# A seventh up group by seven products, the residual's turn on two queues, and a partial sum in free banks of the last round

## The chip, the cores and the metric

The kernel runs on one core of a Trainium2 chip. The metric is device time in microseconds (us) of one execution; lower is better. The engines are TensorE (PE), VectorE (DVE), ScalarE (ACT), GpSimd (POOL) and SyncE (SP). DMAs are issued here from SP's queue, from GpSimd's and, rarely, from ScalarE's.

## The reference

Two residual layers on 512 rows of width 1024 in float32: a mixer (banded attention in layer 0, a gated linear recurrence in layer 1), then a dense MLP. Only the MLP is touched:

```
def sq_relu_mlp(h, w1, w2):
    z = jax.nn.relu(jnp.einsum('bsd,df->bsf', h, w1))
    return jnp.einsum('bsf,fd->bsd', z * z, w2)

for layer in range(DEPTH):
    hn = rmsnorm(h, norm_mix[layer])
    ...
    h = h + mix
    h = h + sq_relu_mlp(rmsnorm(h, norm_mlp[layer]), mlp_w1[layer], mlp_w2[layer])
return rmsnorm(h, norm_final)
```

w1 is 1024 x 4096 and w2 4096 x 1024, each 16 MB, so an MLP reads 32 MB of weights.

## The kernel before

**A product.** Every float32 matmul is made of three (mm3, L273 to L276): high by high part (L274), low by high (L275), high by low (L276). Weights come by DMA into raw tiles, and each is split into a high part `wh` by a cast on ScalarE (L178) and a low part `wl` by a subtraction on VectorE (L181). The split parts live in a ring of five.

**The planner.** `plan` is a list of weight pieces in the order of use. `want` (L210) hands out the next piece and first calls `fetch` (L152) for the next three or four. `fetch` issues the DMA of a plain piece, makes the sums of weights that a piece needs, splits it, and, keyed by the kind of the piece, issues the loads of later pieces (`load_up`, `load_down`). So the place of a piece in the plan sets both when its casts and when later loads are issued.

**Seven products.** A group of 512 features is the product of two 2 x 2 block matrices, and `group` (L764 and after) computes it by seven block products instead of eight, in the order u11, us1, us2, u12, us3, us4, u22. The blocks of w1 are 512 x 256. us1 is the sum of two blocks and is made by a load and a load that accumulates, issued on GpSimd (L136, `kept` tiles). us2 is made on VectorE from u11 and us1. us3 is the block u11 with a block accumulated on it by a DMA of GpSimd (L163); it can be issued once us2 has read u11. us4 is made on VectorE (L166). Each product is 24 matmuls of 128x256. The copies `S.copy(b6, b1)`, `S.copy(v, b5)` and `S.copy(u, b6)` stand between them: b6 starts as a copy of b1 after the first product, and the third and later products accumulate on it.

**Down products.** The down side of a round p takes two groups (1024 features) and is made by seven products as well, named by their weights 11, t1, 22, 21, t2, t3, t4 in the plan and 11, s1, s4, 12, s2, s3, 22 by their activations in `round_`. Sums of blocks of w2 are made by DMAs b<-b on GpSimd (L123, L174). The activations are sums too, made by `opening` and `sums`, and split by `split` (L851 on ScalarE, L852 on VectorE). `read` (L741) adds a finished bank to the residual d on VectorE, scaled by the row's factor `rq` or `nrq`.

**The order of an MLP.** (1) Eight plain columns, `up(0, 0)` to `up(0, 7)`, 1024 features. Each is 24 matmuls of 128x512, two relus and two squares on ScalarE (L754, L755). (2) Rounds 0 to 3. In rounds 0 to 2 each of the seven down products is followed by two of the fourteen up products of the next round's two groups. Round 3 has no up products. Its end is `turns` (layer 0) or `ends` (layer 1).

**What lies between the columns.** After column 0, `turn` (L723) transposes the residual on VectorE into two tiles `turned` (L727) and sends 32 DMAs of 64 KB to d, all on SP (L734). After the columns 1 to 5 the operands of the groups are scaled and split (`scaled`, `right`, `right_split`). After column 5 the eight squares of d (`squares`, L949, 128x512 with a row sum) give the lengths of the rows, and after column 6 rq is made from them. The loads for round 0 and the next group are issued after the columns 4 to 6.

In round 3 the step 11 writes banks X; after s4 the kernel copies X to Y (`S.copy(Y[t], X[t])`, L899), since step 12 goes on in Y what 11 began, while s2 goes on in X. Y is read before that for s1 and s4.

Of the kernel before, what the change touches and what calls it, by code (L numbers as in the profile page):

```python
# [40 lines left out]
def trunk(ctx: ExitStack, tc: tile.TileContext, xT, cols, gfin, win, wqkv, wo, rwin, rga, rgx, rwo, w1, w2, out):  # L41
# [10 lines left out]
    def mmp(name):  # L52
        return ps.tile([P, T], F32, name=name, tag="mm")
# [66 lines left out]
    def first_sum(key):  # L120
        if key in down:
            for h in range(2):
                G.dma_start(raws["12", h], raws["11", h], accum_op=ALU.add)  # L123
# [14 lines left out]
    def fetch():  # L138
        i = state["next"]
        state["next"] += 1  # L140
        kind, nk, key = plan[i]
        H = wsp.tile([P, 1024], F32R, name=f"wh{i}", tag="wh")
        L = wsp.tile([P, 1024], F32R, name=f"wl{i}", tag="wl")
        n, half = 1024, nk
        if kind[:5] == "plain":
            n = nk * sum(src.shape[1] for src in key)
            raw = wraw.tile([P, 1024], F32, name=f"wr{i}", tag=f"wr{state['plain'] % 3}")
            state["plain"] += 1
            rv = raw[:, :n].rearrange("p (k c) -> p k c", k=nk)
            c0 = 0  # L150
            for n_, src in enumerate(key):
                w = src.shape[1]  # L152
                queue = nc.scalar if i == 0 and n_ else nc.sync
                queue.dma_start(rv[:, :, c0 : c0 + w], rows(src))
                c0 += w
        elif kind[0] == "u":
            nk = 4
            following = (key[0], key[1] + 1)
            if kind == "us2":
                raws["us2"] = wraw.tile([P, 1024], F32, name=f"us2_{key[0]}{key[1]}", tag=f"wr{(state['base'] + 2) % 3}")  # L160
                V.tensor_add(raws["us2"], raws["u11"], raws["us1"])
                raws["us3"] = raws["u11"]
                G.dma_start(four(raws["us3"]), rows(upper[key]["21"]), accum_op=ALU.add)  # L163
            if kind == "us4":
                raws["us4"] = raws["u12"]
                V.tensor_add(raws["us4"], raws["us4"], raws["us2"])  # L166
            raw = raws[kind]
        else:
            nk = 2
            following = (key[0], key[1] + 1)  # L170
            raw = raws[{"t1": "12", "t2": "22", "t3": "11", "t4": "21"}.get(kind, kind), half]
            if kind == "t2":
                V.tensor_add(raw, raw, raws["12", half])
                G.dma_start(raws["21", half], raw, accum_op=ALU.add)  # L174
            if kind == "t3":
                V.tensor_sub(raw, raws["22", half], raw)
        if i:
            S.copy(H[:, :n], raw[:, :n])  # L178
        else:
            start_.append(V.tensor_copy(H[:, :n], raw[:, :n]))  # L180
        low = V.tensor_sub(L[:, :n], raw[:, :n], f(H[:, :n]))  # L181
        if not i:
            start_.append(low)
        if kind == "plain_":
            state["base"] = state["plain"] % 3
            load_up((nk_layer[i], 0), "11")
            load_up((nk_layer[i], 0), "12")
        elif kind == "us2":
            load_up(following, "s1")
        elif kind == "us3":  # L190
            load_up(following, "11")
        elif kind == "us4":
            load_up(following, "12")
        elif kind == "u22":
            load_up(following, "22")
        elif kind == "t2" and half:
            load_down(following, "12")
        elif kind == "t3" and half:
            load_down(following, "11")
        elif kind == "t4" and half:  # L200
            first_sum(following)
            load_down(following, "22")
            load_down(following, "21")
        state["ready"].append((nk, H[:, :n].rearrange("p (k c) -> p k c", k=nk), L[:, :n].rearrange("p (k c) -> p k c", k=nk)))
# [31 lines left out]

    def add_mlp(layer):
        starts.append(len(plan))
        for j in range(KT):
            plan.append(("plain" if j < KT - 1 else "plain_", KT, [w1[layer][:, j * P : (j + 1) * P]]))  # L240
        nk_layer[len(plan) - 1] = layer
        for n in range(6):
            c0 = (n + 2) * T
            upper[layer, n] = {
                f"{i + 1}{j + 1}": w1[layer][j * T : (j + 1) * T, c0 + i * U : c0 + (i + 1) * U]
                for i in range(2) for j in range(2)
            }
        for p in range(4):
            down[layer, p] = {
                f"{k + 1}{c + 1}": w2[layer][(2 * p + k) * T : (2 * p + k + 1) * T, c * T : (c + 1) * T]  # L250
                for k in range(2) for c in range(2)
            }
            ups = [("u" + n, 4, (layer, 2 * p + g)) for g in range(2) for n in ("11", "s1", "s2", "12", "s3", "s4", "22")]
            for n, kind in enumerate(("11", "t1", "22", "21", "t2", "t3", "t4")):
                plan.extend((kind, half, (layer, p)) for half in range(2))
                if p < 3:
                    plan.extend(ups[2 * n : 2 * n + 2])
# [409 lines left out]
    def mlp(ly, norm):  # L667
        with ExitStack() as mctx:
# [54 lines left out]
            def turn():  # L723
                blocks = [sr.tile([P, 2, 4, KT, 32], F32, name=f"turned{ly}{h}", tag=f"b{n}2") for h, n in enumerate((1, 2))]
                for k in range(KT):
                    for h in range(2):
                        V.transpose(  # L727
                            blocks[h].rearrange("p t j k a -> p (t j) k a")[:, :, k],
                            hT[k][:, h * U : (h + 1) * U].rearrange("p (n b) -> p n b", b=32),
                        )  # L730
                for h in range(2):
                    for i in range(4):
                        for j in range(4):
                            nc.sync.dma_start(  # L734
                                res[32 * j : 32 * j + 32, 2 * h : 2 * h + 2, i // 2, (i % 2) * U : (i % 2 + 1) * U],
                                blocks[h][32 * i : 32 * i + 32, :, j].rearrange("p t k a -> p t (k a)"),
                            )
# [8 lines left out]
            def up(p, j):  # L746
# [15 lines left out]
                    for n in (1, 3, 2, 4):  # L762
                        right(n)
                if j == 3:  # L764
                    right_split(1)
                    right_split(3)
                if j == 4:
                    right_split(2)
                    opening(0)
                    load_down((ly, 0), "11")  # L770
                if j == 5:
                    right_split(4)
                    state["kept"] = per.tile([P, 2, 1024], F32, name=f"kept{ly}", tag="hx1")
                    load_up((ly, 0), "s1")
                    load_down((ly, 0), "12")
                    first_sum((ly, 0))
                if j == 5:
                    for t in range(4):
                        for c in range(2):
                            squares(t, c)  # L780
                if j == 6:
                    load_up((ly, 0), "22")
                    load_down((ly, 0), "22")
                    load_down((ly, 0), "21")
                    V.tensor_add(rq, fs[:, 0:8:2], fs[:, 1:8:2])
                    V.tensor_scalar(rq, rq, 1.0 / D, EPS, ALU.mult, ALU.add)
                    V.reciprocal(rq, rq)
                    V.tensor_scalar(nrq, rq, -1.0, None, ALU.mult)

            def group(p, g):  # L790
                def piece(bank, op, fresh):
# [81 lines left out]
            def round_(p):  # L873
# [16 lines left out]
                def step(name, bank, fresh, t0, c):  # L890
                    if p < 3:
                        product(name, bank, fresh)
                    for t in range(2):
                        if p == 3:
                            product(name, bank, fresh, ts=(t,))
                        if name != "11":
                            read(bank[t], t0 + t, c)
                        if name == "s4":
                            S.copy(Y[t], X[t])  # L899
                    give(low[name][1])  # L900

                ups = (x for g in range(2) for x in group(p + 1, g)) if p < 3 else iter(range(14))
# [1 line left out]
                def rise(n):  # L904
                    for _ in range(n):
                        next(ups)

                step("11", X, True, 0, 0)
                rise(2)
                split("s4", p)  # L910
# [3 lines left out]
                step("s4", Y, False, 0, 1)  # L914
                rise(2)
                split("s2", p)
                step("12", Y, False, 0, 0)
                rise(2)
                split("s3", p)
                step("s2", X, False, 0, 1)  # L920
# [120 lines left out]
                S.activation(dt[3, 1][:, HI], dt[3, 1][:, HI], AF.Copy, scale=total(3))  # L1041
                store(3, 1, nc.scalar)

            for j in range(KT):
                up(0, j)
            sums(0, False)
            sums(0, True)
            for p in range(4):
                round_(p)
            state["ahead"] = 4  # L1050
# [208 lines left out]
```

## Time and profile before

| | us |
|---|---|
| median of 3 runs | 1042.24 (1040.31 to 1042.85) |
| the profiled execution | 1041.71 |
| its span | 1039.9 |
| TensorE busy | 1025.5 (99%) |
| VectorE busy | 863.0 (83%) |
| ScalarE busy | 659.3 (63%) |
| GpSimd busy | 68.7 (7%) |

The mean granted clock of TensorE is 0.997 of full speed. The plain columns of layer 0 run from 244.61 to 288.15. A row of the timeline gives the start, the duration, the engine with the line, and the operation; in brackets stands the idle time of the engine before it and what ended that. Matmuls overlap in the pipeline, so the price of one is the distance of starts (or a window's length divided by its count), not its own duration.

### The profile page before, as it was taken

Reading aid. Unit: us, or ns where it says so; the run is one execution under the profiler, and the core shown is the slowest. Engines: PE = TensorE matmul, PEld = TensorE weight load, DVE = VectorE, ACT = ScalarE, POOL = GpSimd, SP = SyncE. Lnnn points to the kernel's source line nnn. Section 1 sums busy time; section 2 is a strip of 40 time slices with the busy share of each in tenths; the row PEclk is TensorE's granted clock in tenths of the full one; section 3 lists DMA queues with packets and bytes.
Section 4 is the critical chain, followed back from the end, with each engine's and each line's share of the span. In section 5 each row is a group of like instructions: output and inputs, shape, how many; then the busy total and the mean of one; then the engine's idle time right before and its main releaser. Section 6 shows DMA issues by size and latency. Waiting matters only on the chain.

```text
span 1039.9 us, 14946 instructions
## 1 busy us (share of the span) xinstructions
PE 1025.5 (99%) x5618; PEld 890.4 (86%) x5618; DVE 863.0 (83%) x1216; ACT 659.3 (63%) x1024; POOL 68.7 (7%) x84
## 2 busy tenths in 40 slices
PE   9999999999999999999999999999999999999997
PEld 8888888888889999999988788888889999999985
DVE  7998778969479889689699989988289789789697
ACT  7666556647556567566557686656566566566565
POOL 1000000000111111111000000000111111011000
PEclk9999999999999999999999999999999999999999
DMA  8444354243768738837613422173758738737413
GB/s 273 114 127 137 82 158 126 62 140 98 226 123 222 194 71 220 205 61 202 183 21 94 141 68 73 51 222 104 235 107 223 203 62 222 203 62 202 122 41 102
DMA packets 126248, 145.22 MB, mean 140 GB/s; under 512 B 6240, under 2 KB 98400, under 8 KB 126176
## 3 DMA queue, kind: packets, MB, share of 16 engines
q1 hardware_dynamic: 108320, 114.18, 35.4%
q0 software_dynamic: 17280, 29.36, 16.5%
q8 instruction: 44, 0.72, 0.3%
q10 hardware_dynamic: 576, 0.72, 0.2%
q14 instruction: 28, 0.23, 0.1%
HBM read 116.98 MB, written 2.10 MB: 115 GB/s over the span
## 4 chain that ended last, share of the span: by engine, by line
PE 82%; DVE 9%; DMA 4%; issue 2%; SPq 2%; ACT 1%; DVEq 0%; POOL 0%; ACTq 0%; POOLq 0%
PE m L276 8%; PE m L275 8%; PE m L274 8%; PE x L274 4%; PE x L275 4%; PE x L276 4%; PE y L276 4%; PE y L274 4%; PE y L275 4%; DVE wl L181 3%; DMA b<-b 2%; PE x L500 2%; PE wo L274 1%; PE wo L275 1%; PE ro L275 1%
## 5 line engine op out<-in xcount | busy, mean ns | idle before, releaser
L181 DVE TENSOR_TENSOR wl<-b,wh 128x1024 fp32r<-128x1024 f32 x112 | 136.3, 1223 | 42.8 <-ACT wh L178 42.5
L178 ACT CAST wh<-b 128x1024 fp32r<-128x1024 f32 x112 | 117.1, 1051 | 85.7 <-PE m L275 44.2
L276 PE MATMUL m<-rH,wl 128*128 128x256 f32 x384 | 108.6, 283 | 0.0
L275 PE MATMUL m<-rL,wh 128*128 128x256 f32 x384 | 108.6, 283 | 0.0
L274 PE MATMUL m<-rH,wh 128*128 128x256 f32 x384 | 108.6, 283 | 0.0
L178 ACT CAST wh<-wr 128x1024 fp32r<-128x1024 f32 (+1 forms) x73 | 75.0, 1031 | 45.2 <-PE wo L275 11.7
L181 DVE TENSOR_TENSOR wl<-wr,wh 128x1024 fp32r<-128x1024 f32 (+1 forms) x74 | 87.8, 1190 | 16.0 <-ACT wh L178 15.6
L276 PE MATMUL m<-hnH,wl 128*128 128x256 f32 x288 | 81.6, 283 | 0.0
L275 PE MATMUL m<-hnL,wh 128*128 128x256 f32 x288 | 81.6, 283 | 0.0
L274 PE MATMUL m<-hnH,wh 128*128 128x256 f32 x288 | 81.4, 283 | 0.0
L275 PEld LDWEIGHTS m<-rL,wh 128*128 128x128 f32 x384 | 73.7, 192 | 1.2
L274 PEld LDWEIGHTS m<-rH,wh 128*128 128x128 f32 x384 | 73.6, 192 | 1.2
L276 PEld LDWEIGHTS m<-rH,wl 128*128 128x128 f32 x384 | 73.6, 192 | 0.0
L178 ACT CAST wh<-u 128x1024 fp32r<-128x1024 f32 x48 | 50.4, 1050 | 27.8 <-PE x L276 16.5
L181 DVE TENSOR_TENSOR wl<-u,wh 128x1024 fp32r<-128x1024 f32 x48 | 58.6, 1221 | 4.1 <-ACT wh L178 4.1
L275 PEld LDWEIGHTS m<-hnL,wh 128*128 128x128 f32 x288 | 55.2, 192 | 0.7
L274 PEld LDWEIGHTS m<-hnH,wh 128*128 128x128 f32 x288 | 55.1, 191 | 0.7
L276 PEld LDWEIGHTS m<-hnH,wl 128*128 128x128 f32 x288 | 55.2, 192 | 0.0
L274 PE MATMUL y<-wh,hs 128*128 128x512 f32 x128 | 50.6, 395 | 1.8 <-DVE d L741 1.4
L274 PE MATMUL x<-wh,h 128*128 128x512 f32 (+1 forms) x132 | 50.9, 386 | 1.3 <-DVE d L1030 1.3
L276 PE MATMUL y<-wh,ls 128*128 128x512 f32 x128 | 50.2, 392 | 1.9 <-DVE ls L852 1.9
L276 PE MATMUL x<-wh,l 128*128 128x512 f32 (+1 forms) x132 | 50.9, 385 | 0.0
(373 smaller groups left out, 2964.5 us busy)
## 6 DMA issues: line engine op xcount, KB each, us to landing
b<-in_w SPq DMA_DIRECT2D x64, 512.0 KB, 5.8
b<-b POOLq DMA_DIRECT2D x32, 512.0 KB, 7.3
u<-in_w SPq DMA_DIRECT2D x24, 512.0 KB, 5.0
kept<-in_w SPq DMA_DIRECT2D x24, 512.0 KB, 5.3
wr<-in_wqkv SPq DMA_DIRECT2D x20, 512.0 KB, 4.1
wr<-in_w SPq DMA_DIRECT2D x16, 512.0 KB, 4.3
wr<-in_rwin SPq DMA_DIRECT2D x16, 512.0 KB, 4.0
kept<-in_w POOLq DMA_DIRECT2D x12, 512.0 KB, 5.9
```

What stands on the lines that cost most here:

```text
L178: S.copy(H[:, :n], raw[:, :n])
L181: low = V.tensor_sub(L[:, :n], raw[:, :n], f(H[:, :n]))
L274: PE.matmul(acc, WH, XH, start=start, stop=False, skip_group_check=more)
L275: PE.matmul(acc, WH, XL, start=False, stop=False, skip_group_check=more)
L276: PE.matmul(acc, WL, XH, start=False, stop=stop, skip_group_check=more)
L500: PE.transpose(b[:, c : c + P], pt[:, seg[t] + kt * P : seg[t] + (kt + 1) * P], ident)
```

## The change

1. The second 512 features are no longer four plain columns but a group of seven products, `group(0)`. The plan has four plain columns, then the seven pieces, then the rounds; the groups of the rounds are numbered one higher. The fourth column is now `plain_`, so u11 and u12 of group 0 are loaded before the MLP begins. us2 and u22 of group 0 no longer load the next group's first pieces; a new function `first` does, and it also issues the loads of the down weights between the pieces.
2. All four `right_split` come after column 3. The squares and rq go into `lengths`, called at the end of `first`, after the group and the first sums.
3. `turn` issues every second DMA on GpSimd: 16 on SP, 16 on GpSimd.
4. In round 3 the copy of X goes to two fresh banks Z, right after step 11, and step 12 accumulates there.

The core of the diff:

```diff
-        elif kind == "us2":
+        elif kind == "us2" and key[1]:
             load_up(following, "s1")
...
-        elif kind == "u22":
+        elif kind == "u22" and key[1]:
             load_up(following, "22")
...
-        for j in range(KT):
-            plan.append(("plain" if j < KT - 1 else "plain_", KT, [w1[layer][:, j * P : (j + 1) * P]]))
+        for j in range(4):
+            plan.append(("plain" if j < 3 else "plain_", KT, [w1[layer][:, j * P : (j + 1) * P]]))
...
+        plan.extend(group(0))
...
-            ups = [("u" + n, 4, (layer, 2 * p + g)) for g in range(2) for n in ("11", "s1", "s2", "12", "s3", "s4", "22")]
+            ups = group(2 * p + 1) + group(2 * p + 2)
...
-                            nc.sync.dma_start(
+                            (G if j % 2 else nc.sync).dma_start(
...
+            def lengths():
+                for t in range(4):
+                    for c in range(2):
+                        squares(t, c)
+                V.tensor_add(rq, fs[:, 0:8:2], fs[:, 1:8:2])
...
+            def first():
+                state["kept"] = sr.tile([P, 2, 1024], F32, name=f"kept0{ly}", tag="b21")
+                load_up((ly, 0), "s1")
+                load_up((ly, 0), "22")
+                for j in range(4):
+                    up(0, j)
+                state["kept"] = per.tile([P, 2, 1024], F32, name=f"kept{ly}", tag="hx1")
+                load_down((ly, 0), "11")
+                load_down((ly, 0), "12")
+                first_sum((ly, 0))
+                here = group(0, 1)
+                next(here)
+                opening(0)
+                load_up((ly, 1), "s1")
+                next(here)
+                load_down((ly, 0), "22")
+                for n in range(4):
+                    next(here)
+                load_down((ly, 0), "21")
+                load_up((ly, 1), "22")
+                next(here)
+                sums(0, False)
+                sums(0, True)
+                lengths()
...
-                        if name == "s4":
-                            S.copy(Y[t], X[t])
+                        if name == ("s4" if p < 3 else "11"):
+                            S.copy(Z[t], X[t])
...
+                Z = Y if p < 3 else [mmp(f"z{ly}{t}") for t in range(2)]
...
-                step("12", Y, False, 0, 0)
+                step("12", Z, False, 0, 0)
...
-            for j in range(KT):
-                up(0, j)
-            sums(0, False)
-            sums(0, True)
+            first()
```

How instructions move, at the places that matter below. GpSimd's queue where the MLP of layer 0 begins, before (L363 and L364 end the attention's bias; kept is the tile for us1, u_00 the block that becomes us3, b_00 the down weights):

```order
L363 COPY bias_1816<-bias_1816 128x256 x4
L364 MEMSET bias_1816 64x4x64
L136 DMA kept_2839<-in_w 128x4x256
L123 DMA b_00_2842<-b_00_2801 128x1024 x2
L163 DMA u_00_2757<-in_w 128x4x256
```

The same place after:

```order
L367 COPY bias_1816<-bias_1816 128x256 x4
L368 MEMSET bias_1816 64x4x64
L136 DMA kept_2553<-in_w 128x4x256
L738 DMA d_2550<-turned_2588 32x2x256 x8
L738 DMA d_2550<-turned_2589 32x2x256 x8
L163 DMA u_00_2502<-in_w 128x4x256
L123 DMA b_00_2765<-b_00_2762 128x1024 x2
```

The sixteen turn DMAs now stand ahead of us3's accumulating load. GpSimd's queue at the MLP of layer 1, after:

```order
L136 DMA kept_6871<-in_w 128x4x256
L163 DMA u_10_6798<-in_w 128x4x256
L738 DMA d_6868<-turned_6906 32x2x256 x8
L738 DMA d_6868<-turned_6907 32x2x256 x8
L123 DMA b_10_7083<-b_10_7080 128x1024 x2
```

Here us3's load stands ahead of the turn. ScalarE in layer 0, before, at the sixth plain column (u_2808 is its bank, wr the eighth column's raw weights, b_00 the first down weights, dsq a square of d):

```order
L949 ACTIVATE dsq_2859,fs<-d_2546 128x512
L754 ACTIVATE a_0_2786<-u_2808 128x256
L754 ACTIVATE a_0_2789<-u_2808 128x256
L178 CAST wh_2751<-wr_2753 128x1024
L178 CAST wh_2804<-b_00_2801 128x1024
L755 ACTIVATE a_0_2786<-a_0_2786 128x256
L755 ACTIVATE a_0_2789<-a_0_2789 128x256
L949 ACTIVATE dsq_2861,fs<-d_2546 128x512
```

The same engine after, from the cast of us3 to the copy of b1 (m_2770) to b6 (m_2772):

```order
L178 CAST wh_2812<-u_00_2502 128x1024
L758 ACTIVATE a_0_2582<-u_2723 128x256
L758 ACTIVATE a_0_2585<-u_2723 128x256
L759 ACTIVATE a_0_2582<-a_0_2582 128x256
L759 ACTIVATE a_0_2585<-a_0_2585 128x256
L867 CAST h_2806<-a_0_2582 128x1024
L178 CAST wh_2846<-u_00_2504 128x1024
L838 COPY m_2772<-m_2770 128x512
```

wh_2812 is the cast of us3, which needs GpSimd's load. Behind it stand the relus and squares of column 3, the split h of the first activations, the cast of us4 and the copy. The squares of d have moved to a later place.

TensorE in round 3 of layer 0, where the last product in the banks y for s1 ends and s4's begins, before:

```order
L276 MATMUL y_5232<-wh_5235,ls_0_5196 128x512
L274 MATMUL y_5232<-wh_5235,hs_5195 128x512
L275 MATMUL y_5232<-wl_5236,hs_5195 128x512
L276 MATMUL y_5232<-wh_5235,ls_0_5196 128x512
L274 MATMUL y_5231<-wh_5239,hs_5267 128x512
L275 MATMUL y_5231<-wl_5240,hs_5267 128x512
L276 MATMUL y_5231<-wh_5239,ls_0_5268 128x512
```

The same place after (z are the new banks):

```order
L280 MATMUL y_5318<-wh_5323,ls_0_5282 128x512
L278 MATMUL y_5318<-wh_5323,hs_5281 128x512
L279 MATMUL y_5318<-wl_5324,hs_5281 128x512
L280 MATMUL y_5318<-wh_5323,ls_0_5282 128x512
L278 MATMUL z_5321<-wh_5365,h_5395 128x512
L279 MATMUL z_5321<-wl_5366,h_5395 128x512
L278 MATMUL z_5322<-wh_5365,h_5395 128x512
L278 MATMUL y_5317<-wh_5327,hs_5357 128x512
L279 MATMUL y_5317<-wl_5328,hs_5357 128x512
```

Three matmuls of step 12 (z) now stand between the last of s1 and the first of s4. Before, s4's followed s1's directly, and step 12 came after all of s4.

More of the change, by code (lines that the diff above doesn't have):

```diff
@@ L238, in add_mlp @@
         starts.append(len(plan))
-        for j in range(KT):
-            plan.append(("plain" if j < KT - 1 else "plain_", KT, [w1[layer][:, j * P : (j + 1) * P]]))
+        for j in range(4):
+            plan.append(("plain" if j < 3 else "plain_", KT, [w1[layer][:, j * P : (j + 1) * P]]))
         nk_layer[len(plan) - 1] = layer
-        for n in range(6):
-            c0 = (n + 2) * T
+        for n in range(7):
+            c0 = (n + 1) * T
             upper[layer, n] = {
@@ L247, in add_mlp, with group @@
             }
+        def group(n):
+            return [("u" + x, 4, (layer, n)) for x in ("11", "s1", "s2", "12", "s3", "s4", "22")]
+        plan.extend(group(0))
         for p in range(4):
@@ L764, in up @@
                 if j == 3:
[L765 to L788, printed above, removed]
+                    for n in (1, 3, 2, 4):
+                        right_split(n)
@@ new lines, in lengths @@
+            def lengths():
[3 more added lines that the diff above has]
+                V.tensor_add(rq, fs[:, 0:8:2], fs[:, 1:8:2])
+                V.tensor_scalar(rq, rq, 1.0 / D, EPS, ALU.mult, ALU.add)
+                V.reciprocal(rq, rq)
+                V.tensor_scalar(nrq, rq, -1.0, None, ALU.mult)
+            def first():
[22 more added lines that the diff above has]
+                lengths()
```

## Prediction

> **What bounds the kernel now.** I read the page first, then who waits for whom on TensorE, then windows over the stretches that the change touches, then the chain of waits in the one place where TensorE stops for long. The page:
>
> ```profile
> span 1039.9 us, 14946 instructions
> PE 1025.5 (99%) x5618; PEld 890.4 (86%) x5618; DVE 863.0 (83%) x1216; ACT 659.3 (63%) x1024; POOL 68.7 (7%) x84
> PE 82%; DVE 9%; DMA 4%; issue 2%; SPq 2%; ACT 1%; DVEq 0%; POOL 0%; ACTq 0%; POOLq 0%
> ```
>
> TensorE is the bound: 99% busy, 82% of the chain. A change can win only by taking matmuls away or by filling the little time in which TensorE stands still. The waits of TensorE in the two MLPs:
>
> ```profile
> PE y L276 <- DVE ls L852: 1.9, 2, 1.6
> PE y L274 <- DVE d L741: 1.4, 2, 0.7
> PE y L274 <- ACT hs L851: 0.4, 1, 0.4
> ```
>
> The columns are total us, times and longest. The first and third are the start of round 0 (the first down products wait for the split of their activations), the second is round 3. Windows give the prices (the columns after the stretch: its length, then busy us and instruction count of PE, PEld, DVE, ACT and POOL, then the granted clock, the DMA share and GB/s):
>
> ```profile
> 244.61:266.38 21.77, 21.77 (x97) 18.03 (x96) 17.63 (x25) 17.37 (x34) 0.00 (x0) 1.00 0.32 81
> 266.38:288.15 21.77, 21.77 (x98) 18.04 (x96) 7.91 (x10) 12.13 (x29) 3.25 (x3) 1.00 0.88 262
> 308.85:314.54 5.69, 5.69 (x49) 5.69 (x48) 5.69 (x7) 3.54 (x4) 0.00 (x0) 1.00 0.08 24
> 296.34:303.09 6.75, 4.76 (x21) 3.97 (x20) 6.51 (x6) 5.02 (x6) 1.30 (x1) 0.75 0.56 90
> ```
>
> Row 1 is the first four plain columns of layer 0: 96 weight loads, so 96 matmuls of 128x512, 21.77 us, 0.2267 us each. Row 3 is two of the seven products: 48 matmuls of 128x256 in 5.69 us, 0.119 us each. Row 4 is the start of round 0, with TensorE idle for 6.75 - 4.76 = 1.99 us and the clock at 0.75. In it start 15 matmuls of 0.119 and 4 of 0.2267, 2.69 us of work, so 4.06 us are lost: 1.99 idle, 0.25 x 6.75 = 1.69 to the lower clock, the rest in restarts. The chain of waits tells why (start, us, what):
>
> ```profile
> 260.60 0.59 SPq L734
> ...
> 269.55 0.60 SPq L734
> ...
> 274.92 6.84 DMA b<-in_w
> 282.53 9.73 DMA b<-b
> 292.41 1.06 ACT wh L178
> 298.15 1.14 DVE ls L852
> 299.34 0.55 PE y L276
> ```
>
> SP's queue issues the 32 residual transfers one after another until 270; only then come the MLP weights that stand behind them, their sum on GpSimd's queue lands at 292, and the split for the first down products is late.
>
> **The change, part by part.**
>
> *Seven products for the second 512 features.* Removed per layer: four columns, 21.77 us. Added: seven products of 24 matmuls at 0.119, 20.0 us. Both lie on TensorE, so 1.78 us per layer, **3.55 us** in all, if the new pieces are fed in time.
>
> *The residual's turn on two queues.* The cost of an issue on either queue, and the time to landing:
>
> ```profile
> L734 SPq DMA_DIRECT2D d<-turned x64: 585/595/1550, 249.5 to 735.9; - x64
> L163 POOL DMA_DIRECT2D u<-in_w x12: 1302/1312/1321, 291.7 to 948.9; - x12
> L123 POOL DMA_DIRECT2D b<-b x16: 856/884/1010, 282.5 to 970.1; - x16
> 282.53 1.82 POOL L123 DMA_DIRECT2D b<-b  x2
> u<-in_w POOLq DMA_DIRECT2D x12, 512.0 KB, 6.2
> ```
>
> SP takes 595 ns for a turned block (rows are min/median/max ns). GpSimd issues none in this trace, so its price has bounds: 0.60 us (as SP's) and 1.31 us (its dearest kind). A transfer of kind u<-in_w has 512 runs of 256 numbers, b<-b 128 runs of 1024, a turned block 64 runs of 256; it is nearest to b<-b, two of which take 1.82 us, 0.91 each. I take 0.87 us: 16 of them from 249.55 last till 263.5. On SP 16 go instead of 32, and the weights behind them leave some 10 us earlier. This ends the cause of the 4.06 us.
>
> But GpSimd's queue in layer 0 now holds the turn ahead of us3's accumulating load (the order shows it): issued at 263.5 instead of as soon as its operand is free, it lands 6.2 us later, at 269.7. On ScalarE the cast of that weight stands in a row ahead of the last plain column's relus, the cast h, the cast for us4, and the copy b1 to b6, on which the third piece (us2) accumulates. The prices:
>
> ```profile
> 272.03 0.66 ACT L754 ACTIVATE a<-u 128x256 f32<-128x256 f32 x2 [2.62 <-PE u L276]
> 272.57 0.72 ACT L755 ACTIVATE a<-a 128x256 f32<-128x256 f32 x2
> 273.19 0.63 ACT L949 ACTIVATE dsq<-d 128x512 f32<-128x512 f32 x1
> 273.71 0.20 ACT L949 ACTIVATION_READ_ACCUMULATOR dsq<-d 128x1 f32 x1
> 273.80 0.62 ACT L949 ACTIVATE dsq<-d 128x512 f32<-128x512 f32 x1
> 278.01 1.05 ACT L178 CAST wh<-wr 128x1024 fp32r<-128x1024 f32 x1
> 278.95 1.06 ACT L178 CAST wh<-b 128x1024 fp32r<-128x1024 f32 x1
> L822 ACT COPY m<-m 128x512 f32<-128x512 f32 x6 | 3.5, 581 | 0.0
> ```
>
> Start to start, a cast takes 0.95, the two relus and two squares of a column 1.16, one dsq 0.61; the copy takes 0.58. From 269.7: 0.95 + 1.16 + 0.95 + 0.95 + 0.58 = 4.6, so the copy ends at 274.3. TensorE ends the four columns at 244.61 + 21.77 = 266.38, u11 and us1 at 272.1, and then needs it: **2.15 us** of new stall. With 0.60 us an issue, or anything up to 0.73, there is none; with 1.31 it is (1.31 - 0.87) x 16 = 7.0 longer. A stall of 1.99 us brought the half clock in the row above; here it may or may not, so I add half of the 1.69: **3.0 us** in place of 4.06, a gain of **1.1** in layer 0.
>
> By the Trainium skill (TensorE: Matmul & The Clock Gate, Part 1) the clock halves only after an idle window of some 3.4 us. By that rule the 0.85 would drop out; the row at 296.34 speaks against it, since 1.99 us of idle time were enough.
>
> In layer 1 the order on GpSimd is the other way round, us3's load ahead of the turn, so this stall isn't there.
>
> *Sums, squares and the first down weights after the group.* Eight dsq move off a stretch where ScalarE had slack (17.37 busy of 21.77 in the first row, 12.13 in the second) to the end of group 0, on the way to the first weight of t1, for which y waits. From the end of us3's piece ScalarE has 4 casts and 14 operations of 512: 4 x 0.95 + 14 x 0.62 = 12.5 us, then VectorE's wl, some 1.4: 14.1 with the start. TensorE has two more pieces (5.71), b11 (24 of 0.2267, 5.44) and the next group's first piece (2.86), so it needs that wl at 14.24. The margin is 0.1 us. Were a dsq taken with the 0.20 read of the accumulator instead, the eight (0.2 each) would bring 1.6 us more, a stall of 1.5. I take 0.1 in layer 1, where it stands against this:
>
> ```profile
> 765.63 0.40 PE L275 MATMUL y<-wl,hs 128*128 128x512 f32 x1
> 766.38 0.50 PE L276 MATMUL y<-wh,ls 128*128 128x512 f32 x1 [0.36 <-DVE ls L852]
> 766.72 0.28 PE L274 MATMUL m<-rH,wh 128*128 128x256 f32 x1
> ```
>
> Two matmuls in 1.09 us instead of 0.45: 0.64 lost now, so a gain of **0.5**. In layer 0 the 3.0 us stall ahead of it leaves ScalarE time to catch up.
>
> *Partial sum in free banks.* Round 3, where nothing fills in between:
>
> ```profile
> 537.94 0.39 PE L276 MATMUL y<-wh,ls 128*128 128x512 f32 x1
> 539.03 0.47 PE L274 MATMUL y<-wh,hs 128*128 128x512 f32 x1 [0.70 <-DVE d L741]
> 539.34 0.39 PE L275 MATMUL y<-wl,hs 128*128 128x512 f32 x1
> 525.58:552.50 26.92, 26.22 (x123) 21.69 (x122) 26.88 (x26) 16.51 (x19) 1.74 (x2) 1.00 0.21 40
> ```
>
> Two matmuls in 1.40 instead of 0.45: 0.95 lost to the read of y by VectorE, once in each layer (the row of waits has it twice). Step 12 no longer needs that bank, and the order puts three of its matmuls, 0.68 us, ahead of s4's. That would fill 0.68 of 0.95 per layer. But VectorE works 26.88 of 26.92 us here, so some of the time may come back as a wait later. I take 0.45 per layer, **0.9** in all; the bounds are 0 and 1.9.
>
> *Sum.* 3.55 + 1.1 + 0.5 + 0.9 = 6.05 us. The profiled execution took 1041.71 (span 1039.9, 1.81 around it), 0.53 under the median of 1042.24. From the median: **1036.2**.
>
> **The rivals.** A difference of 0.3%, 3.1 us, is about what a measurement of this kernel can tell from no change.
>
> *No stall at us3.* GpSimd issues 64 short runs in 0.73 us or less, or the load lands early. Then all 4.06 us come back: 3.55 + 4.06 + 0.5 + 0.9 = 9.0, **1033.2**. For it: the short runs, and SP's 0.60. Against: the cheapest issue of GpSimd in the rows is 856 ns.
>
> *The chains of VectorE and ScalarE give it back.* The squares stall y for 1.5 us in both layers, and round 3 gains nothing: 3.55 + (4.06 - 3.0 - 1.5) + (0.64 - 1.5) + 0 = 2.25, **1040.0**. For it: 26.88 of 26.92, and a margin of only 0.1. Against: in the rows of waits TensorE waits 0.4 us for ScalarE, no more.
>
> *GpSimd's turn is dear (slower).* At 1.31 us an issue, us3's load leaves at 270.5 and lands at 276.7, the stall is 9.2 us, and the clock goes with 1.7: layer 0 loses 6.8, in all 3.55 + 0.5 + 0.9 - 6.8 = -1.9, **1044.1**, still within what can be told. The kernel gets measurably slower when the load lands later than about 278: at 1.4 us an issue, or at 1.31 with a landing like the slowest of its kind. That slowest row is
>
> ```profile
> DMA to landing us min/median/max: 5.9/6.2/8.4
> ```
>
> for u<-in_w of GpSimd, and gives 2.2 more, **1046.3**. For it: 12 loads at 1.30 without exception. Against: b<-b at 0.88 shows that the price goes with the runs.
>
> *GpSimd is locked out while VectorE works.* Each issue would then also wait out an instruction of VectorE, 1.14 us by the row of ls L852, and 16 issues take 16 x 2.0 = 32 us instead of 14: the stall is 2.15 + 18, with the clock 22, and the sum 3.55 + 0.5 + 0.9 + 4.06 - 22 = -13, about **1055**. Against it: min and max of L163 are 19 ns apart although VectorE is busy for 83% of the span. The Trainium skill (SBUF — State Buffer, A bandwidth-pool intuition that's wrong (but worth ruling out)) states such a lock for a copy of VectorE, with 620 ns growing to 3100. By that figure 16 issues take 50 us, an estimate; the rows of L163 don't agree with it for the subtractions that run here.
>
> **How the numbers follow.** Forecast (a stall of 1 to 4 us at us3) 0.45, nearly all of it faster by over 0.3% (0.42), the rest the same (0.03). No stall 0.22, faster. Give-back 0.17: 0.05 faster, 0.12 the same. Dear turn 0.13: 0.06 the same, 0.07 slower. Locked out 0.03, slower. Together 0.69 faster, 0.21 the same, 0.10 slower. The range begins below the second case, with round 3 at its full 1.9 (1032.2), and reaches up into the dear turn, to 1042.8; outside lie about 0.05 below and 0.12 above.
>
> **What would show it.** Right: 16 turn rows on GpSimd at about 0.87 us; us3's load issued at about 263.5; a wait of TensorE for the copy of b6 near 272 of about 2 us; y of round 0 without a wait over 0.5 in layer 1; the 0.70 waits for d gone; a layer's up part 1.78 shorter. Wrong: turn rows of 1.3 us or of varying length, a wait of TensorE over 5 us in layer 0, waits for wl of t1 over 1 us in both layers, or a new wait in round 3 as long as the one that went.

## The result, and the profile after

The changed kernel takes 1050.76 us (median of 4 runs, 1049.87 to 1051.97); the kernel before, on the same chip, 1042.55. The ratio is 1.0083 with a 95% interval of 1.0064 to 1.0102: slower by 8.2 us, where 6 us faster was forecast. The profiled execution took 1050.44, its span is 1048.7. The page of the changed kernel:

```profile
span 1048.7 us, 15295 instructions
PE 1023.1 (98%) x5762; PEld 894.3 (85%) x5762; DVE 876.6 (84%) x1230; ACT 667.2 (64%) x1020; POOL 91.0 (9%) x120
PE 81%; DVE 9%; DMA 5%; issue 2%; SPq 1%; ACT 1%; POOL 0%; DVEq 0%; ACTq 0%; POOLq 0%
```

TensorE is busy for 2.4 us less than before, in a span that is 8.8 us longer. So the work did shrink, and the loss is waiting. The waits of TensorE:

```profile
PE m L278 <- DVE a L820: 12.7, 2, 6.7
PE x L278 <- DVE d L1047: 1.7, 1, 1.7
```

None of the three waits in the MLPs that the prediction lists is left: not the splits `ls` and `hs` at the start of round 0, not the read of d in round 3. In their place stands one that wasn't there, twice, once in each layer. The last of the seven new products (u22, which accumulates on the bank b6) waits for VectorE to read that bank (`a<-m,v`, L820). The windows around it, in layer 0 and layer 1:

```profile
283.93:294.20 10.27, 3.62 (x18) 3.42 (x17) 6.98 (x8) 3.36 (x8) 1.29 (x1) 0.67 0.44 151
756.03:765.25 9.22, 3.19 (x16) 2.98 (x15) 6.96 (x7) 2.93 (x7) 1.19 (x1) 0.63 0.47 159
```

In 10.27 and 9.22 us TensorE starts some 16 and 14 matmuls of 0.119, 1.9 and 1.7 us of work. So 8.4 and 7.5 us are lost, 15.9 together: 12.7 idle, the rest mostly the clock, which was still halved (0.51) for 3.3 us behind the first stop and 2.9 us behind the second; 0.67 and 0.63 are means that take in the stops. Why did the read come so late? VectorE's timeline (start, duration, line, operation, and in brackets the idle time before it and what ended that):

```profile
271.34 1.22 DVE L181 TENSOR_TENSOR wl<-u,wh 128x1024 fp32r<-128x1024 f32 x1
285.57 1.23 DVE L161 TENSOR_TENSOR us<-u,kept 128x1024 f32<-128x1024 f32 x1 [13.01 <-DMA kept<-in_w]
286.71 1.22 DVE L181 TENSOR_TENSOR wl<-kept,wh 128x1024 fp32r<-128x1024 f32 x1
287.85 2.35 DVE L181 TENSOR_TENSOR wl<-b,wh 128x1024 fp32r<-128x1024 f32 x2
290.12 0.68 DVE L820 TENSOR_TENSOR a<-m,v 128x512 f32<-128x512 f32 x1
```

VectorE stood idle for 13 us with work behind it. At the head of its queue was the sum us2 of the *next* group (u_01 plus kept), a weight that TensorE needs only in round 0. It waited for kept's accumulating load. Behind it stood the splits of u22 and b11 and the read that frees the bank; their operands were there. TensorE finished its sixth piece at 283.93 and had nothing to do. GpSimd's timeline and two rows of the transfers issued between 262 and 286 (KB each, median us to landing):

```profile
250.64 8.57 POOL L738 DMA_DIRECT2D d<-turned  x16 [17.22 <-ACT h L686]
259.19 1.39 POOL L163 DMA_DIRECT2D u<-in_w  x1
268.86 0.89 POOL L123 DMA_DIRECT2D b<-b  x1 [8.27 <-DMA b<-in_w]
270.74 0.85 POOL L123 DMA_DIRECT2D b<-b  x1 [0.99 <-DMA b<-in_w]
272.28 1.31 POOL L136 DMA_DIRECT2D kept<-in_w  x1 [0.70 <-DMA kept<-in_w]
```

```profile
u<-in_w SPq DMA_DIRECT2D x2, 512.0 KB, 11.9
kept<-in_w POOLq DMA_DIRECT2D x1, 512.0 KB, 13.3
```

The load was issued at 272.28 and landed 13.3 us later; the median of its kind before was 5.9. In the same stretch the DMA engines are full (the share is 1.05 in the first row, of the changed kernel, and 0.76 in the second, of the kernel before):

```profile
262.00:286.00 24.00, 22.21 (x167) 21.15 (x165) 9.47 (x9) 12.49 (x21) 3.05 (x3) 1.00 1.05 263
```

```profile
262.00:286.00 24.00, 24.00 (x108) 19.89 (x107) 8.54 (x11) 14.38 (x37) 3.25 (x3) 1.00 0.76 237
```

A full share alone doesn't make such a load slow, though: from 274 to 286 the share of the kernel before is 1.08 as well, and kept's load, issued at 281.10, landed after 8.7 us there.

That is the picture; the experiments test it. In the order of instructions the sum stands ahead of the read in the changed kernel, and the order was not written by hand: with the whole turn on SP it comes out the other way. VectorE in layer 0 of the changed kernel:

```
L161 TENSOR_TENSOR us_01_3107<-u_01_2816,kept_2761 128x1024
L181 TENSOR_TENSOR wl_2879<-kept_2553,wh_2878 128x1024
L181 TENSOR_TENSOR wl_2910<-b_00_2762,wh_2909 128x1024
L181 TENSOR_TENSOR wl_2940<-b_00_2762,wh_2939 128x1024
L820 TENSOR_TENSOR a_0_2937<-m_2772,v_2774 128x512
```

and with the turn on SP alone, all else the same:

```
L181 TENSOR_TENSOR wl_2879<-kept_2553,wh_2878 128x1024
L181 TENSOR_TENSOR wl_2910<-b_00_2762,wh_2909 128x1024
L181 TENSOR_TENSOR wl_2940<-b_00_2762,wh_2939 128x1024
L820 TENSOR_TENSOR a_0_2937<-m_2772,v_2774 128x512
L181 TENSOR_TENSOR wl_2975<-u_01_2816,wh_2974 128x1024
L820 TENSOR_TENSOR a_0_2937<-m_2771,u_2773 128x512
L161 TENSOR_TENSOR us_01_3107<-u_01_2816,kept_2761 128x1024
```

In the program's text the sum comes after all of these. The order that runs is planned from the program by a tool (not the `plan` of the kernel), and with the split turn, which lets the loads start earlier, it puts the sum first. That the earlier loads are its reason is argued from these two orders.

### The profile page after: what moved, and what is told of

Same layout as the page of the kernel before. It is cut to its first block, busy times and chain, and to the rows that moved or that the text cites. A ratio compares the mean times of both kernels' runs of the same rounds, so it can differ in the third digit from the quotient of the medians.

```text
span 1048.7 us, 15295 instructions
## 1 busy us (share of the span) xinstructions
PE 1023.1 (98%) x5762; PEld 894.3 (85%) x5762; DVE 876.6 (84%) x1230; ACT 667.2 (64%) x1020; POOL 91.0 (9%) x120
## 4 chain that ended last, share of the span: by engine, by line
PE 81%; DVE 9%; DMA 5%; issue 2%; SPq 1%; ACT 1%; POOL 0%; DVEq 0%; ACTq 0%; POOLq 0%
PE m L278 8%; PE m L280 8%; PE m L279 8%; PE x L279 5%; PE x L280 5%; PE x L278 5%; PE y L278 4%; PE y L279 3%; PE y L280 3%; DMA kept<-in_w 3%; DVE wl L181 3%; PE x L504 2%; PE wo L278 1%; PE wo L279 1%; PE v L278 1%
## 5 line engine op out<-in xcount | busy, mean ns | idle before, releaser
L278 PE MATMUL m<-rH,wh 128*128 128x256 f32 x448 | 127.4, 284 | 12.7 <-DVE a L820 12.7
L280 PE MATMUL m<-rH,wl 128*128 128x256 f32 x448 | 127.1, 284 | 0.0
L279 PE MATMUL m<-rL,wh 128*128 128x256 f32 x448 | 127.0, 284 | 0.0
L278 PEld LDWEIGHTS m<-rH,wh 128*128 128x128 f32 x448 | 86.3, 193 | 14.3 <-DVE a L820 13.1
L280 PE MATMUL m<-hnH,wl 128*128 128x256 f32 x336 | 95.0, 283 | 0.0
L279 PE MATMUL m<-hnL,wh 128*128 128x256 f32 x336 | 95.0, 283 | 0.0
L278 PE MATMUL m<-hnH,wh 128*128 128x256 f32 x336 | 94.9, 282 | 0.0
L279 PEld LDWEIGHTS m<-rL,wh 128*128 128x128 f32 x448 | 86.4, 193 | 1.2
L280 PEld LDWEIGHTS m<-rH,wl 128*128 128x128 f32 x448 | 86.3, 193 | 0.0
L279 PE MATMUL x<-wl,h 128*128 128x512 f32 (+1 forms) x132 | 50.9, 386 | 0.0
```

The costliest lines, as they stand in the source:

```text
L278: PE.matmul(acc, WH, XH, start=start, stop=False, skip_group_check=more)
L279: PE.matmul(acc, WH, XL, start=False, stop=False, skip_group_check=more)
L280: PE.matmul(acc, WL, XH, start=False, stop=stop, skip_group_check=more)
```

## The experiments

Theory A: the loss is a queue's. The sum waits at the head of VectorE, and what is ready stands behind it. Rivals: the weights are simply late, wherever the sum stands (B); the turn on GpSimd makes them late (C).

**add_late.** One ordering is added; no transfer changes.

```diff
-                V.tensor_add(raws["us2"], raws["u11"], raws["us1"])
+                ins = V.tensor_add(raws["us2"], raws["u11"], raws["us1"])
+                if key[1] == 1:
+                    after(ins, state["read"])
...
-                        V.tensor_add(c, bank, more)
+                        state["read"] = V.tensor_add(c, bank, more)
```

> The changed kernel with one ordering added: the sum us2 of the next group (u_01 plus kept on VectorE) comes behind the two reads of group 0's banks instead of ahead of them. All transfers stay as they are. Theory A (the 6.8 and 6.7 us of TensorE are a queue's: the sum waits 13 us for kept's accumulating load at the head of VectorE, and the read that frees the bank stands behind it): the two waits go, 15.9 us with the half clock, so about 1050.8 - 15.9 = 1035; the load still lands about 13 us after its issue. Rival B (the weights come too late because the DMA engines are full): the stall moves to the next piece that needs kept or u_01, and the time stays above 1043.

Measured: 1035.26 us, ratio to before 0.9948 (0.9930 to 0.9965). VectorE in layer 0:

```profile
280.68 0.69 DVE L822 TENSOR_TENSOR a<-m,v 128x512 f32<-128x512 f32 x1 [0.70 <-PE m L282]
281.64 1.22 DVE L183 TENSOR_TENSOR wl<-u,wh 128x1024 fp32r<-128x1024 f32 x1 [0.27 <-ACT wh L180]
283.56 0.69 DVE L822 TENSOR_TENSOR a<-m,u 128x512 f32<-128x512 f32 x1 [0.70 <-PE m L282]
285.29 1.23 DVE L161 TENSOR_TENSOR us<-u,kept 128x1024 f32<-128x1024 f32 x1 [1.04 <-DMA kept<-in_w]
```

The read now follows TensorE at once, and the sum runs at 285.29, hardly earlier than in the changed kernel (285.57). The load is as slow as it was (issued at 271.47, landed by 285.3), and it costs nothing. Theory A holds and B falls: the medians are 15.5 us apart (14 by the ratios), against 15.9 lost in the two windows.

**turn_sp.** The changed kernel with `nc.sync.dma_start(` in `turn` for all 32.

> The changed kernel with all 32 transfers of the turn on SP again. The order then has the sum us2 behind the read of the bank in both layers. Theory A: no wait of TensorE for that read; SP is busy with the turn some 10 us longer, so down weights come later, with up to 3 us of stall at the start of round 0 in layer 0: 1035 to 1039. Rival C (the split turn is what makes the loads late, the order does not matter): about the same time, but then add_late must stay slow. Rival B: slower than the changed kernel, above 1051, since the loads are issued later still.

Measured: 1058.43 us, ratio 1.0160 (1.0142 to 1.0177), outside what A expected here and what C did. It is the time that B gave for this kernel. The order of VectorE is the good one, and the wait for the bank is gone, but another has come:

```profile
PE y L278 <- ACT wh L178: 18.9, 2, 10.3
```

SP's turn lasts 23.4 us, and the loads behind it start late. Kept's load is issued by GpSimd at 283.59 and lands at 296. ScalarE's cast of it, which stands at the same place in add_late and waited 1.5 us there, now holds up ScalarE for 9.4:

```profile
249.72 23.39 SPq L738 DMA_DIRECT2D d<-turned  x32
```

```profile
286.01 0.62 ACT L966 ACTIVATE dsq<-d 128x512 f32<-128x512 f32 x1
...
296.07 1.04 ACT L178 CAST wh<-kept 128x1024 fp32r<-128x1024 f32 x1 [9.35 <-DMA kept<-in_w]
```

So the split of the turn is needed by the new group: with the read of b6 ahead of the sum on both sides it is worth 1058.4 - 1035.3 = 23 us. (In layer 1 of turn_sp the sum still stands ahead of the second read; ScalarE waits 0.8 us more for that read, after 9.9 for kept.) The split is also what turns the order of VectorE to the bad one. So in this kernel the weights are too late, as B has it; in the changed kernel, where they start 11 us earlier, add_late shows that they aren't. C falls as it was put: the split makes no load late; it lets them start earlier, and the planned order then puts the sum first.

**kept_first, held, acc_ahead.** Three kernels keep the sum at the head of VectorE and try to make its load land earlier. kept_first issues kept's load ahead of the b12 loads:

```diff
                 load_down((ly, 0), "11")
+                load_up((ly, 1), "s1")
                 load_down((ly, 0), "12")
...
-                load_up((ly, 1), "s1")
```

> The changed kernel with kept's load for the next group issued ahead of the down weights b12 and their sums; the sum us2 stays ahead of the reads on VectorE. Theory A with the load's wait in GpSimd's queue: the accumulating load leaves some 4 to 5 us earlier and each wait of 6.8 shrinks to 2 or 3: about 1041. If the full DMA engines alone set when it lands: it lands as late as before, about 1050.

held lets b22, b21 and kept's second half wait until that load has landed:

```diff
+            if name == "22" and key[1] == 0:
+                G.tensor_copy(both[:, h, 0:1], state["kept"][:, 0, 0:1])
...
+            if name == "22" and key[1] == 1:
+                G.tensor_copy(raw[:, 0:1], state["kept"][:, 0, 0:1])
```

> The changed kernel, VectorE's order as in it, but the loads of b22, b21 and of kept's second half wait until kept's accumulating load has landed (a one-column copy on GpSimd makes them wait; the loads overwrite it). If the 13 us of that load come from full DMA engines, it lands in 7 to 9 us, and the two waits of TensorE shrink from 6.8 to under 2.5: 1038 to 1042. If such a load always takes 13 us at this place, or GpSimd is the cause: the waits stay, about 1050.

acc_ahead also puts the accumulating load ahead of both b12 sums on GpSimd (`first_sum` moves behind the fourth piece of the group as well, which these lines don't show):

```diff
-                G.dma_start(raws["12", h], raws["11", h], accum_op=ALU.add)
+                ins = G.dma_start(raws["12", h], raws["11", h], accum_op=ALU.add)
+                if key[1] == 0:
+                    after(ins, state["acc"])
...
-            G.dma_start(four(raw), rows(upper[key]["22"]), accum_op=ALU.add)
+            state["acc"] = G.dma_start(four(raw), rows(upper[key]["22"]), accum_op=ALU.add)
```

> The changed kernel, the sum us2 at the head of VectorE as in it, but kept's accumulating load stands ahead of the two sums b12 on GpSimd, where it stood behind them. Theory D (transfers of GpSimd's queue move one after another: in the changed kernel the load's packets wait some 7 us behind the two sums, then take 6): it lands 6 to 8 us after its issue and no longer ends the wait; what comes last is then the load of u_01 on SP, which lands near 281, so waits of 2 to 4 us stay in each layer: 1038 to 1043. Rival (the DMA engines are full, and every load takes 12 to 13 us there): it lands 12 to 13 us after its issue, and the time is that of kept_first, 1043, or worse.

Measured, with the wait of TensorE and the landing of that load (us):

| kernel | us | ratio to before (95%) | wait for the read, two layers | landing of kept's load of GpSimd, layer 0 |
|---|---|---|---|---|
| changed kernel | 1050.76 | 1.0083 (1.0064 to 1.0102) | 12.7 | 13.3 |
| kept_first | 1043.33 | 1.0022 (1.0012 to 1.0033) | 7.7 | 13.2 |
| held | 1043.86 | 1.0026 (1.0015 to 1.0037) | 7.1 | 12.2 |
| acc_ahead | 1042.82 | 1.0014 (1.0002 to 1.0026) | 6.4 | 11.4 |

The rows of acc_ahead (the last is of all such loads, min/median/max):

```profile
PE m L280 <- DVE a L824: 6.4, 2, 3.5
DVE us L163 <- DMA kept<-in_w: 9.3, 1, 9.3
```

```profile
DMA to landing us min/median/max: 5.9/6.0/11.4
```

Each starts the load 1.6 to 3.0 us earlier. acc_ahead also takes 1.9 us off its landing, held 1.1 and kept_first 0.1; none makes it fast. Held's landing of 7 to 9 us failed, and so did theory D's 6 to 8. The times tell little: kept_first is 2 us above its 1041, held lies between its two forecasts, and acc_ahead lies in the range of theory D, but just below the 1043 of its rival too. In layer 1 of acc_ahead (and of kept_first) the wait ends with u_01's load, which SP issues:

```profile
750.63 1.23 DVE L163 TENSOR_TENSOR us<-u,kept 128x1024 f32<-128x1024 f32 x1 [9.82 <-DMA u<-in_w]
```

The packets in the traces tell where the time of kept's load goes, and they bear out the first half of theory D. The rows below give a queue's packets, MB and share of the 16 engines; q0 holds GpSimd's transfers, q1 SP's. In the changed kernel, from 272.3 to 279.3 (two rows) and from 279.4 to 285.2 (the third):

```profile
q0 software_dynamic: 251, 0.96, 71.8%
q1 hardware_dynamic: 616, 0.84, 35.4%
q0 software_dynamic: 556, 0.58, 61.2%
```

A packet of a b12 sum has 4 KB, one of kept's load 1 KB. So in the first stretch q0 moves the two sums. The 512 packets of the load begin at 279.39, 7.1 us after its issue, and end at 285.17. In acc_ahead the sums come behind the load, yet its first packet moves at 275.68, 5.1 us after its issue. From 271.8 to 275.6 q0 moves nothing and SP's loads fill the engines:

```profile
q1 hardware_dynamic: 814, 1.05, 94.6%
```

The load's own packets take 5.8 or 5.9 us in all four kernels. So most of the 13.3 us is a wait of 7.1 behind the two sums and a transfer of 5.8; with the sums out of the way another wait takes the place of the first. That SP's loads cause that other wait is argued: no kernel here takes both away.

**turn_alone and z_alone.** The kernel before with one part of the change each: `(G if j % 2 else nc.sync)` in `turn`, and the banks Z in round 3 with their copy.

> The kernel before with the second part alone: the residual's turn on two queues. The 4.06 us lost at the start of round 0 in layer 0 came from weights that stood behind the turn on SP, so they go, and 0.64 in layer 1: up to 4.7 us faster, 1037 to 1038 where before is at 1041.5. If something else fills the gap: no change.

> The kernel before with the third part alone: in round 3 the partial sum goes to two free banks. The two waits of 0.70 for the read of d go; of 0.95 lost in each layer 0.2 stays, so 1.5 us faster at most, 0.9 as forecast: 1041.0 to 1041.6. If VectorE gives it back: no change, 1042.5.

turn_alone: 1037.47 us, ratio 0.9964 (0.9951 to 0.9978), 4.3 us faster; the waits for `ls` and `hs` are gone in both layers. z_alone: 1041.19, ratio 0.9994 (0.9982 to 1.0006), no difference.

**add_late_no_z.** add_late with `S.copy(Y[t], X[t])` after s4 and step 12 in Y, as before.

> The kernel of add_late without the third part: round 3 copies X into Y after s4 again. The waits of 0.70 for the read of d come back, 0.95 lost instead of 0.19 in each layer: 1.5 us slower than add_late, about 1036.8; about 0.3 slower if z_alone's small difference is the true size.

Measured: 1034.77 us, ratio 0.9937 (0.9925 to 0.9950), not slower than add_late. Its trace has the waits of round 3 that add_late's hasn't, and both spans are 1033.5:

```profile
PE y L280 <- DVE d L747: 1.4, 2, 0.7
```

In add_late the first y of s4 starts 0.31 after the last z instead of 0.23; but 30 us later, between the layers, TensorE waits where add_late_no_z runs on, for the first activations of the next layer:

```profile
533.51 0.40 PE L280 MATMUL z<-wh,h 128*128 128x512 f32 x1
533.82 0.50 PE L280 MATMUL y<-wh,hs 128*128 128x512 f32 x1
...
563.86 0.49 PE L280 MATMUL xb<-hnH,wh 128*128 128x512 f32 x1 [0.21 <-ACT hnH L300]
...
566.07 0.51 PE L281 MATMUL xb<-hnL,wh 128*128 128x512 f32 x1 [0.23 <-DVE hnL L301]
```

These two waits hand back 0.44 of the 0.75 us that the round wins in layer 0; by 603 us the same matmuls (`ga`) start within 0.1 us of each other in both traces. In layer 1 about half comes back at the end of the kernel, where x waits for the read of d for 1.7 us in add_late and for 1.3 in add_late_no_z.

**lengths_later.** add_late still lost 0.85 and 0.83 us at the start of round 0, for the split of t1's weight behind the squares on ScalarE:

```profile
PE y L281 <- DVE wl L183: 1.1, 2, 0.6
```

The squares are moved behind the first down product in the program:

```diff
-                lengths()
...
                 step("11", X, True, 0, 0)
+                if p == 0:
+                    lengths()
                 rise(2)
```

> The kernel of add_late with the eight squares and the row factors behind the first down product of round 0 in the program, so that the cast of the first weight of t1 stands ahead of five squares on ScalarE. The 0.85 and 0.83 us that y still loses at the start of round 0 for the low part of that weight go: 1.5 us faster than add_late, about 1033.8. If the row factors then come late for the first reads of d: as slow as add_late or slower.

Measured: 1033.59 us, ratio 0.9931 (0.9919 to 0.9944); that wait is gone from the trace. It has the lowest median here, 8.2 us below the kernel before (7.2 by the ratio); its interval overlaps that of add_late, so the gain over add_late itself isn't shown by the times.

## Why the prediction was wrong, point by point

- **The step that failed** is "if the new pieces are fed in time". The prediction checked it at one place, the copy to b6 for the third piece (us2), and let the other six pass. The last piece needs b6 read by VectorE, and the prediction never followed VectorE's row of instructions through the group. What the runs showed in its place: the sum us2 of the next group stands ahead of that read and waits for its loads. Had these been priced at their medians (kept's 5.9 us, from 272.28), the sum would have started near 278 and nothing would be late; at the 13.3 measured (13.6 in layer 1) TensorE stood for 6.7 and 6.0 us. Both the place and the size were missed, and no rival had them, though one of the prediction's own signs of being wrong came, a wait of TensorE over 5 us in layer 0. The price is 15.9 us by the windows; add_late, which only puts the sum behind the reads, is 15.5 us faster.
- **Seven products**: right. The four columns take 21.78 us and six pieces 17.09 from their first start to their last (266.84 to 283.93, 143 steps of 0.1195), so 2.87 each. That is 1.70 us a layer, about 3.4 of the 3.55.
- **The turn on GpSimd**: the price was wrong in the good direction. The rows of the changed kernel are

```profile
L738 SPq DMA_DIRECT2D d<-turned x32: 585/600/1823, 250.0 to 734.1; - x32
L738 POOL DMA_DIRECT2D d<-turned x32: 539/547/700, 250.6 to 732.1; - x32
```

  0.55 us an issue, below both bounds (0.60 and 1.31) that were taken for it. us3's load left at 259.19 instead of 263.5, and the stall of 2.15 us at the third piece didn't come: the rival without a stall was right on this point, and the 4.06 us of layer 0 came back in full. turn_alone shows the part by itself, 4.3 of the 4.7 in both layers.
- **The squares**: the margin of 0.1 was too good. Where nothing else stalls (add_late), y loses 0.85 and 0.83, between the 0.1 taken and the 1.5 of the rival.
- **Banks Z**: the waits went as described (0.19 lost instead of 0.95), and the caution wasn't enough: nothing that can be measured is left of 1.5 us, in two comparisons. The sentence that VectorE works 26.88 of 26.92 us there was the one to follow.
- **The sum without the new wait** is close: 6.05 forecast, 6.2 measured for add_late against its own kernel before (1041.5; 5.4 by the ratio, 3.6 to 7.3). That is luck in part, since errors cancel: 4.06 instead of 1.1 in layer 0, against Z and the squares.
- **GpSimd locked out by VectorE**: no sign of it. While the sixteen issues ran at 0.54 each, VectorE was busy for 11.90 of 12 us:

```profile
250.00:262.00 12.00, 12.00 (x55) 9.94 (x54) 11.90 (x12) 9.74 (x17) 9.95 (x17) 1.00 0.74 176
```

## What to carry to other kernels

When a change lets loads start earlier, read where the planned order puts the instructions that consume them: an in-order engine that waits for a load holds back everything behind it, and a piece that nobody needs yet can stop the bound engine. Follow each engine's whole row through a new stage, and price a wait for a load with what stands ahead of that load in its queue, not at the median of its kind. The repair was one ordering, worth some 15 us; three repairs of the load itself were worth 6 to 8.

## What the runs showed of the hardware

- An issue from GpSimd of a turned block (64 runs of 256 numbers) takes 0.55 us, less than SP's 0.60, where 512 runs take 1.31 and 128 longer ones 0.88.
- An accumulating load of 512 KB took 13.3 us to land in the changed kernel, where the median of its kind was 5.9 before: its first packet moved 7.1 us after the issue, behind two sums in the same queue, and its packets took 5.8. Two plain loads of the same size took 9.4 and 14.3 there. The DMA share was 1.05; in the kernel before, at 1.08, the same kind of load landed after 8.7.
- After stops of 6.7 and 6.0 us TensorE ran at half clock for another 3.3 and 2.9 us. Before the change, waits of 0.40 and 1.59 us came with a granted clock of 0.75 over 6.75 us, so with some 3.4 us at half clock. The Trainium skill (TensorE: Matmul & The Clock Gate, Part 1) puts the window of the clock gate at 3.4 us. The slow stretch of the kernel before agrees with that length; the waits that were enough for it are shorter than that window.
